# The second layer's feed-forward stage: a lower task rate in its first block, and wider spacing between the steps that write the first output rows

## The chip, the cores and the metric

The kernel runs on one core of one Trainium2 chip. The metric is the device time of one execution in microseconds; the time given for a kernel is the median of its runs. The profile is one further execution, recorded by the hardware profiler, with its own time and its own span from the first to the last instruction.

The core has TensorE (matrix products, with weight loads shown apart as PEld), VectorE (DVE), ScalarE (ACT), GpSimd (POOL) and SyncE (SP). Each works through its own list of instructions, and they wait for each other through semaphores. All transfers between HBM and the on-chip memory of this kernel are issued by SP, one after the other.

## The reference, cut to what matters

The reference is one inference step of a two-layer decoder, on a prompt of 1024 tokens and eight samples of eight tokens, 1088 token columns in all, with a model width of 1024. Each layer mixes tokens, adds the residual and normalises, then runs a feed-forward stage with its own residual and normalisation:

```python
def swiglu_ffn(x, w_in, w_out):
    gate, up = jnp.split(x @ w_in, 2, axis=-1)
    return (jax.nn.silu(gate) * up) @ w_out

xp = deepnorm_residual(xp, mix_p @ w_out[l], ln_mix_g[l], ln_mix_b[l])
xp = deepnorm_residual(xp, swiglu_ffn(xp, w_ffn_in[l], w_ffn_out[l]), ln_ffn_g[l], ln_ffn_b[l])
```

`deepnorm_residual(x, h, g, b)` is a layer norm over the 1024 features of `ALPHA * x + h`, with gain `g` and bias `b`. The hidden width is 2816. The samples' columns `xs` go through the same two lines. After layer 1 (the second) the result is the output `y`.

## The kernel before, in words

**Layout.** The residual stream `mx` is kept transposed: 128 features on the partitions, 8 feature tiles, and 1088 token columns. Columns are cut into three chunks: chunk 0 has 512, chunk 1 has 256 and chunk 2 has 320. To keep float32 accuracy every operand of a product is split into a high and a low part (`wh`, `wl` for weights, `xh`, `xl` for columns), and each product is three matmuls. ScalarE makes the high part of a weight (L169, in `halves`), and VectorE or GpSimd the low one (L172, which is the line of the helper `tt` and so stands for most VectorE and GpSimd work in the profile).

**The feed-forward stage** is `ffn(l, background)`, called once a layer. It has two blocks: block 0 takes chunk 0, block 1 takes chunks 1 and 2. A block goes through the 22 hidden tiles in six groups of four or three. For each hidden tile, `gates` makes seven products of sums of operands (a Strassen-like scheme) into PSUM, each 12 matmuls, and between them evacuates, applies the SiLU, multiplies, and writes the hidden tile `hid`. After each group, `parts` multiplies its hidden tiles with the output weights and `add_part` adds the results into `mx`. The four PSUM banks of one hidden tile come alternately from the pool `pd` (with one called `gp`) and from the pool `gb`. The sums of operands that a block needs are made by the task `combine_x`, which in block 1 may start only when block 0's last gates are done.

**The background tasks.** Work on vectors is written as Python generators, kept in a queue `S` (class `Streams`). The code that emits products calls `S.tick()` after every product of `gates` and after every `add_part`. A tick adds `S.rate` to a credit, and as many steps of tasks as the credit's whole part are emitted:

```python
self.credit = min(self.credit + self.rate, 2 * self.rate + 1)
if self.credit >= 1:
    self.credit -= self._advance(int(self.credit))
```

In one tick a task takes at most one step, tasks at the front first, and among the first three live tasks only. A task that yields `n` is due again `n` ticks later; one that yields 0 is due again at the next tick. A task that yields a condition isn't live until it holds. `S.until(cond)` steps tasks without emitting products until the condition holds.

Which instruction comes first on an engine is settled in two stages: the order in which the code emits it gives its priority, and a planner then places instructions by priority as they become ready, and gives out buffers from the pools.

**Tasks around the change.** `out_proj` queues `norm` for each chunk after the mixing. For chunks 1 and 2 (there `calm` is true) that task waits 14 ticks (`LAZY[0]`), adds up the eight feature tiles in four steps (`lnsum`), squares in four steps (`lnsq`), and after two waits scales the eight tiles in eight steps (L676). These tasks run beside block 0 of `ffn`. The rates are in `RT = (2.3, 3.0, 1.0, 4.25, 4.25, 2.5)`: the main program sets `RT[2]` before layer 0's output projection, which then holds through `ffn(0)`, and `RT[5]` before `ffn(1)`.

**The output rows.** In layer 1, block 1 begins by loading gain and bias rows (`grow`, `brow`) and queues `y_out(0, ...)`. It waits 14 ticks (`LAZY[1]`) and then handles chunk 0's four tiles of 128 tokens one by one through `y_tiles`: two halves, each four transposes into a PSUM bank `ytr`, statistics (L961) and a copy into the tile `yst`; then aggregate (L970), variance (L971) and its power on GpSimd; then two passes on VectorE for each half (L979, L982); then the store to `y_p` (L987) on SP's queue. `yst` comes from the pool `slots` of ten buffers, with the hidden tiles, `grow`, `brow` and part of the raw weights (`rawu`). Chunks 2 and 1 are handled by the same function at the end, without waits between steps. Weight loads are issued by `load_raw` (L249), on the same queue of SP as the stores.

Of the kernel before, what the change touches and what calls it, by code (L numbers as in the profile page):

```python
# [87 lines left out]
def trunk(ctx: ExitStack, tc: tile.TileContext, A: dict, O: dict, g128, g8):  # L88
# [35 lines left out]
    S = Streams(3)  # L124
    LNY = ((1, 5, 2), (3, 11, 5), (4, 7, 2))
    LAZY = (14, 14)
    RT = (2.3, 3.0, 1.0, 4.25, 4.25, 2.5)
# [43 lines left out]
    def tt(out, a, b, op, eng=None):  # L171
        (eng or nc.vector).tensor_tensor(out=out, in0=a, in1=b, op=op)  # L172
# [139 lines left out]
    def piece(ahead):  # L312
        prefetch(1)
        out = ready_pieces.popleft()
        prefetch(ahead)
        return out
# [508 lines left out]
    def ffn(l, background):  # L825
        def gates(blk, f, last):

            n = HALF[blk][1]
            XH, XL = x_sums(blk)
            assert plan[at["next"]][0] == ("sf", l, blk, f)  # L830
            at["next"] += 1

            def prod(i, ps, start, stop):
                wh, wl = piece(PA[0])
                for k in range(4):
                    mm(ps, lhsT=wl[:, k], rhs=XH[:, i, k], start=start and k == 0, stop=False, skip_group_check=True)
                    mm(ps, lhsT=wh[:, k], rhs=XL[:, i, k], start=False, stop=False, skip_group_check=True)
                    mm(ps, lhsT=wh[:, k], rhs=XH[:, i, k], start=False, stop=stop and k == 3, skip_group_check=True)
                S.tick()
                return ps  # L840

            sets["use"] ^= 1
            A_, B_, C_, D_ = (new_bank(i)[:, :n] for i in range(4))
            v, u1, u0 = (rt([P, n], nm) for nm in ("v1", "up1", "up0"))
            hid = slot([P, 2, 2 * n], F32R, "hid")

            def result(i, u, g):

                hs = slice(i * n, i * n + n)
                tt(g, u, g, ALU.mult)  # L850
                acopy(hid[:, 0, hs], g)
                tt(hid[:, 1, hs], g, hid[:, 0, hs].bitcast(F32), ALU.subtract)

            prod(0, A_, True, True)
            acopy(v, A_)
            prod(4, B_, True, True)
            tt(v, v, B_, ALU.add)
            prod(2, C_, True, True)
            tt(u1, v, C_, ALU.add)
            prod(1, D_, True, True)  # L860
            tt(u1, u1, D_, ALU.add)
            prod(3, A_, False, True)
            nc.scalar.activation(A_, A_, AF.Silu)
            prod(5, C_, False, True)
            tt(u0, v, C_, ALU.add)
            result(0, u0, A_)
            prod(6, D_, False, True)
            tt(D_, v, D_, ALU.add)
            nc.scalar.activation(D_, D_, AF.Silu)
            result(1, u1, D_)  # L870
            if last:
                done.add(("gates", l, blk))
            return hid

        def parts(outs, gi, hid, b0):

            sums = []
            for i, (w, m, c) in enumerate(outs):
                c0, n = CH[c]
                ps = new_bank(i)  # L880
                sums.append((w, ps[:, :n], slice(c0 - b0, c0 - b0 + n)))
            for ks in (range(len(hid) - 1), range(len(hid) - 1, len(hid))):
                for (wh, wl), ps, ts_ in sums:
                    for k in ks:
                        first, end = k == 0, k == len(hid) - 1
                        mm(ps, lhsT=wl[:, k], rhs=hid[k][:, 0, ts_], start=first, stop=False)
                        mm(ps, lhsT=wh[:, k], rhs=hid[k][:, 1, ts_], start=False, stop=False)
                        mm(ps, lhsT=wh[:, k], rhs=hid[k][:, 0, ts_], start=False, stop=end)
            for (w, m, c), (_, ps, _) in zip(outs, sums):
                add_part(ps, m, c, gi)  # L890

        def add_part(ps, m, c, gi):
            c0, n = CH[c]
            y = mx[:, m, c0:c0 + n]
            if gi == 0:
                nc.vector.scalar_tensor_tensor(out=y, in0=y, scalar=ALPHA, in1=ps, op0=ALU.mult, op1=ALU.add)
            else:
                tt(y, y, ps, ALU.add)
            S.tick()

        for blk in range(2):
            S.until(lambda: ("xsum", l, blk) in done)
            if l == 1 and blk == 1:
                grow, brow = slot([P, D], F32, "grow"), slot([P, D], F32, "brow")
                dma(grow, A["ln_ffn_g"][1:2, :].to_broadcast([P, D]))
                dma(brow, A["ln_ffn_b"][1:2, :].to_broadcast([P, D]))
                S.add(y_out(0, grow, brow))
            b0 = HALF[blk][0]
            for gi, (f0, f1) in enumerate(GROUPS):
                end = f1 == NF  # L910
                hid = []
                for f in range(f0, f1):
                    hid.append(gates(blk, f, f1 == NF and f == f1 - 1))
                    background()
                if end and blk == 1 and l == 0:
                    S.add(x_parts(0), front=True)
                for ci, cs in enumerate(LAST[l] if end and blk else (BCH[blk],)):
                    sums = [None, None]
                    for m in range(0, KT, 2):
                        ws = weights(("fo", l, blk, gi, ci, m))  # L920
                        outs = [(ws[q], m + q, c) for q in range(2) for c in cs]
                        if m == 0:
                            sets["use"] ^= 1
                            parts(outs[:4], gi, hid, b0)
                        for q in range(2):
                            for i, c in enumerate(cs):
                                if m or len(cs) * q + i >= 4:
                                    parts([(ws[q], m + q, c)], gi, hid, b0)
                                if end and l == 0 and blk:
                                    sums[i] = stat_add(sums[i], m + q, c, nc.vector)  # L930
                                elif end and (m + q) % 4 == 3:
                                    done.add(("y", c, m // 4))
                                    if blk and m < 4:
                                        S.add(y_out(c, grow, brow), front=True)
                    if end and l == 0:
                        for i, c in enumerate(cs):
                            S.add(norm(c, sums[i], 1, l), front=True)
# [10 lines left out]
    def y_tiles(c, tiles, grow, brow):  # L948
# [3 lines left out]
        for half in range(2):  # L952
            yield from wait(("y", c, half))
            hs = slice(half * 512, half * 512 + 512)
            for T, n in tiles:
                if half == 0:
                    st[T], st6[T] = slot([P, D], F32, "yst"), small(12, "yst6")
                b = bank("ytr")
                for i in range(4):
                    transpose(b[:n, i * P:(i + 1) * P], mx[:, half * 4 + i, T * P:T * P + n], ident)  # L960
                nc.vector.bn_stats(out=st6[T][:n, half * 6:half * 6 + 6], in_=b[:n])  # L961
                if end:
                    src[T, half] = b[:n]
                else:
                    acopy(st[T][:n, hs], b[:n])
                    src[T, half] = st[T][:n, hs]
                yield 0
        for T, n in tiles:
            mv, r = small(2, "ymv"), small(2, "yr")
            nc.vector.bn_aggr(out=mv[:n], in_=st6[T][:n].rearrange("p (a s) -> p a s", a=2))  # L970
# [3 lines left out]
        for T, n in tiles:  # L974
            mv, r = st6[T]
            for half in range(2):
                hs = slice(half * 512, half * 512 + 512)
                y, b = st[T][:n, hs], brow[:n, hs]
                nc.vector.scalar_tensor_tensor(out=y, in0=src[T, half], scalar=mv[:n, 0:1], in1=grow[:n, hs],  # L979
                                               op0=ALU.subtract, op1=ALU.mult)  # L980
                if half or c == 0:
                    nc.vector.scalar_tensor_tensor(out=y, in0=y, scalar=r[:n, 0:1], in1=b, op0=ALU.mult, op1=ALU.add)  # L982
                else:
                    nc.scalar.activation(y, y, AF.Copy, scale=r[:n, 0:1])
                    tt(y, y, b, ALU.add, nc.gpsimd)
            if T < 8:
                dma(O["y_p"][0, T * P:(T + 1) * P, :], st[T])  # L987
            else:
                dma(O["y_s"].rearrange("b t d -> (b t) d"), st[T][:64])
            yield 0  # L990
# [756 lines left out]
```

## Time and profile before

| What | Value |
|---|---|
| Median of 3 runs | 2698.9 us (2698.22 to 2705.96) |
| Profiled execution, its own time | 2692.69 us |
| Its span | 2690.9 us |
| Mean granted TensorE clock | 0.992 |
| Layer 1, block 0 of the feed-forward stage | about 1910 to 2247 us of the span |
| Layer 1, block 1 | about 2272 to 2664 us |
| Chunk 0's output rows on VectorE | 2298.5 to 2331 us |

Engine names in rows are PE and PEld (TensorE's products and weight loads), DVE, ACT, POOL and SP. In a row of busy time by stretch stand the stretch, its length, and each engine's busy time with the count of its instructions, then the granted clock, the share of the DMA engines and GB/s. A row of waits reads: the engine, the tile and line that waited, what released it, then the total in us, how often, and the longest. In a row of a group stand the line, engine, operation, tiles and shape with the count, then busy us and the mean ns of one, then the idle time before it. A row for one line or tile has the least, median and longest duration in ns, and the first and last start.

### The profile page before, as it was taken

How to read it: one execution, taken by the hardware profiler on the slowest of the kernel's cores; microseconds unless marked ns; L12 is line 12 of the kernel's file. 1: busy time of each engine (PE TensorE's matmuls, PEld its weight loads, DVE VectorE, ACT ScalarE, POOL GpSimd, SP SyncE). 2: the span in 40 equal slices, each digit the busy share in tenths (PEclk: the TensorE clock that was granted, in tenths of full speed). 3: DMA queues.
4: the chain of work that ended last, by engine and by line, in shares of the span. 5: the costliest groups of instructions: out<-in, count | busy, mean ns of one | idle time of the engine just before them, and what ended most of it. 6: DMA issues, size and time to landing. Idle time of an engine off the chain costs nothing. (4 is left out here: it accounts for less than half of the span.)

```text
span 2690.9 us, 48282 instructions
## 1 busy us (share of the span) xinstructions
PE 2603.3 (97%) x18057; PEld 2351.7 (87%) x18057; DVE 1829.9 (68%) x3843; ACT 1204.7 (45%) x2621; POOL 934.3 (35%) x1118
## 2 busy tenths in 40 slices
PE   8999999999999999999999999989999999899997
PEld 8788888898999989999977777768989998899997
DVE  4454435578777797665775775677887669866666
ACT  4442223344544554444455555544454445344434
POOL 0012223654444443334520111136344444433335
PEclk9999999999999999999999999989999999999998
DMA  7311111223333332333342453542333433433332
GB/s 253 95 41 49 49 56 57 64 86 126 114 120 116 122 114 89 120 114 94 103 132 61 146 163 95 160 141 87 102 99 126 134 110 122 134 114 114 99 98 83
DMA packets 417819, 289.23 MB, mean 107 GB/s; under 512 B 21360, under 2 KB 403120, under 8 KB 415920
## 3 DMA queue, kind: packets, MB, share of 16 engines
q1 hardware_dynamic: 417584, 286.13, 34.5%
q8 instruction: 143, 2.34, 0.3%
q14 instruction: 92, 0.75, 0.1%
HBM read 272.25 MB, written 40.83 MB: 116 GB/s over the span
## 5 line engine op out<-in xcount | busy, mean ns | idle before, releaser
L172 POOL TENSOR_TENSOR wl<-rawu,wh 128x256 fp32r<-128x256 f32 (+1 forms) x560 | 449.8, 828 | 833.1 <-ACT wh L169 744.9
L112 PE MATMUL pd<-xh,wl 128*128 128x256 f32 (+3 forms) x2080 | 673.8, 325 | 10.6 <-DVE up L172 3.9
L112 PE MATMUL pd<-xh,wh 128*128 128x256 f32 (+3 forms) x2080 | 660.3, 318 | 0.0
L112 PE MATMUL pd<-xl,wh 128*128 128x256 f32 (+3 forms) x2080 | 659.3, 317 | 0.2 <-DVE xl L172 0.2
L169 ACT ACTIVATE wh<-raw 128x512 fp32r<-128x512 f32 (+1 forms) x628 | 388.8, 623 | 565.6 <-DVE raw L172 206.0
L112 PEld LDWEIGHTS pd<-xh,wl 128*128 128x128 f32 x2080 | 392.8, 189 | 48.5 <-issue 21.3
L172 DVE TENSOR_TENSOR wl<-raw,wh 128x512 fp32r<-128x512 f32 x460 | 341.3, 745 | 120.1 <-ACT wh L169 116.2
L112 PEld LDWEIGHTS pd<-xl,wh 128*128 128x128 f32 x2080 | 394.5, 190 | 24.5 <-issue 5.8
L112 PEld LDWEIGHTS pd<-xh,wh 128*128 128x128 f32 x2080 | 392.7, 189 | 23.8 <-issue 4.4
L112 PE MATMUL gb<-xh,wl 128*128 128x256 f32 (+1 forms) x1232 | 356.6, 289 | 7.1 <-DVE up L172 3.3
L112 PE MATMUL gb<-xh,wh 128*128 128x256 f32 (+1 forms) x1232 | 355.6, 289 | 0.0
L112 PE MATMUL gb<-xl,wh 128*128 128x256 f32 (+1 forms) x1232 | 352.9, 286 | 0.0
L172 POOL TENSOR_TENSOR wl<-raw,wh 128x256 fp32r<-128x256 f32 x336 | 272.0, 836 | 128.4 <-ACT wh L169 115.5
L169 ACT ACTIVATE wh<-rawu 128x512 fp32r<-128x512 f32 (+1 forms) x280 | 170.8, 614 | 197.0 <-PE gb L112 81.2
L112 PE MATMUL gb<-hid,wh 128*128 128x320 f32 (+2 forms) x1056 | 251.8, 329 | 0.0
L112 PEld LDWEIGHTS gb<-xh,wl 128*128 128x128 f32 x1232 | 231.8, 188 | 10.1 <-DVE wl L172 3.2
L112 PE MATMUL pd<-hid,wh 128*128 128x256 f32 (+2 forms) x1018 | 240.3, 327 | 0.1
L112 PEld LDWEIGHTS gb<-xl,wh 128*128 128x128 f32 x1232 | 233.4, 189 | 0.6 <-DVE xl L172 0.2
L112 PEld LDWEIGHTS gb<-xh,wh 128*128 128x128 f32 x1232 | 231.5, 188 | 0.0
L112 PEld LDWEIGHTS gb<-hid,wh 128*128 128x128 f32 x1056 | 180.3, 189 | 13.9 <-DVE hid L172 0.3
L112 PEld LDWEIGHTS pd<-hid,wh 128*128 128x128 f32 x1018 | 172.5, 189 | 14.2 <-DVE hid L172 0.7
L112 PE MATMUL gb<-hid,wl 128*128 128x512 f32 (+2 forms) x528 | 174.0, 331 | 4.2 <-POOL wl L172 2.1
(321 smaller groups left out, 4724.0 us busy)
## 6 DMA issues: line engine op xcount, KB each, us to landing
rawu<-in_w_ffn_in_dram SPq DMA_DIRECT2D x88, 512.0 KB
raw<-in_w_ffn_in_dram SPq DMA_DIRECT2D x88, 512.0 KB
raw<-in_w_out_dram SPq DMA_DIRECT2D x32, 512.0 KB
raw<-in_w_ffn_out_dram SPq DMA_DIRECT2D x32, 512.0 KB
rawu<-in_w_ffn_out_dram SPq DMA_DIRECT2D x32, 512.0 KB
out_wins_dram<-in_cache_win_kv_g_dram SPq DMA_DIRECT2D x64, 256.0 KB
qb<-scr_q SPq DMA_DIRECT2D x64, 256.0 KB
raw<-in_w_in_a_dram SPq DMA_DIRECT2D x26, 512.0 KB
```

What stands on the lines that cost most here:

```text
L112: return pinned(nc.tensor.matmul(*args, **kw))
L169: nc.scalar.activation(out, in_, AF.Copy, scale=scale)
L172: (eng or nc.vector).tensor_tensor(out=out, in0=a, in1=b, op=op)
```

## The change

Two things are edited. In `ffn`, each block now sets the rate after its operands are there: `RT[5]` = 2.5 in block 1 of layer 1 and `RT[2]` = 1.0 elsewhere. Since `ffn(0)` already ran at 1.0, this alters block 0 of layer 1 alone, from 2.5 to 1.0. In `y_tiles`, for chunk 0 alone, a half that has been transposed is followed by a pause of 4 ticks where it was 0, and a pause of 4 ticks is added after each half's last two passes, ahead of the store.

```diff
         for blk in range(2):
             S.until(lambda: ("xsum", l, blk) in done)
+            S.rate = RT[5] if l and blk else RT[2]
             if l == 1 and blk == 1:
...
                     acopy(st[T][:n, hs], b[:n])
                     src[T, half] = st[T][:n, hs]
-                yield 0
+                yield 4 if c == 0 else 0
         for T, n in tiles:
...
                     nc.scalar.activation(y, y, AF.Copy, scale=r[:n, 0:1])
                     tt(y, y, b, ALU.add, nc.gpsimd)
+                if c == 0:
+                    yield 4
             if T < 8:
                 dma(O["y_p"][0, T * P:(T + 1) * P, :], st[T])
```

## The prediction

> **What bounds the kernel now.** I read the page's totals first, then the busy time by stretch, then TensorE's list of waits in the stretches where it is not full.
>
> ```profile
> span 2690.9 us, 48282 instructions
> PE 2603.3 (97%) x18057; PEld 2351.7 (87%) x18057; DVE 1829.9 (68%) x3843; ACT 1204.7 (45%) x2621; POOL 934.3 (35%) x1118
> ```
>
> TensorE sets the end, so only its holes can be won. The change touches layer 1's feed-forward stage alone, and its two blocks begin at about 1910 and 2272 us. The first row below lies in layer 1's first block, the second at the same work in layer 0, the third in layer 1's second block where the first rows of output are made, the fourth just behind it.
>
> ```profile
> core 0: us, PE busy (x) PEld busy (x) DVE busy (x) ACT busy (x) POOL busy (x), PEclk, DMA share, GB/s
> 1936.00:2012.00 76.00, 65.08 (x431) 59.09 (x430) 63.90 (x121) 37.15 (x81) 32.90 (x40) 0.98 0.32 100
> 632.00:708.00 76.00, 71.64 (x488) 65.97 (x487) 66.18 (x131) 40.16 (x88) 33.20 (x40) 0.98 0.36 114
> 2298.00:2336.00 38.00, 31.14 (x225) 29.17 (x225) 35.31 (x67) 16.36 (x33) 19.81 (x21) 1.00 0.48 153
> 2336.00:2400.00 64.00, 64.00 (x485) 64.00 (x484) 41.92 (x81) 27.45 (x53) 23.18 (x30) 1.00 0.36 115
> ```
>
> TensorE is idle for 76 − 65.08 = 10.92 us in layer 1's first block, for 4.36 us at the same work in layer 0, and for 38 − 31.14 = 6.86 us beside the output rows. VectorE is 93% busy in that third stretch. With VectorE at 41.92 / 64 = 65%, TensorE has no hole. So the two holes worth having are 10.9 and 6.9 us. What ends them, in the same order (layer 1's first block, layer 0's, the output rows):
>
> ```profile
> PE pd L112 <- DVE up L172: 3.5, 2, 2.1
> PE lnm L112 <- DVE lnsum L172: 2.9, 2, 2.6
> PE pd L112 <- ACT hid L169: 2.3, 1, 2.3
> PE pd L112 <- POOL wl L172: 2.2, 1, 2.2
> ```
> ```profile
> PE gb L112 <- POOL wl L172: 1.9, 1, 1.9
> PE gb L112 <- DVE up L172: 1.2, 2, 0.9
> PE gb L112 <- ACT hid L169: 0.6, 1, 0.6
> ```
> ```profile
> PE gb L112 <- DVE up L172: 1.9, 1, 1.9
> PE pd L112 <- POOL wl L172: 1.5, 1, 1.5
> PE pd L112 <- ACT hid L169: 1.3, 1, 1.3
> PE gb L112 <- ACT yst L169: 1.1, 1, 1.1
> PE gp L112 <- DVE up L172: 1.0, 1, 1.0
> ```
>
> In each, the products wait for evacuations and weight parts that stand behind other work on VectorE. No DMA is among the releasers.
>
> **Part 1: the pace in the first block.** At each tick the queue of tasks gets `rate` steps of credit. In layer 1's first block the rate falls from 2.5 to 1.0, which is what layer 0 has throughout. The live tasks there are the two `norm` tasks of chunks 1 and 2 alone; `combine_x(1, 1)` waits for the last gates, and with one live task whose steps are one tick apart, either rate gives one step a tick. At 2.5 both norms step at every tick; at 1.0 they share one step. No operation is added or removed. What it spreads is seen in VectorE's timeline and in the norms' scaling at L676, layer 1 first and then layer 0:
>
> ```profile
> 1942.18 3.67 DVE L172 TENSOR_TENSOR lnsum<-lnsum,mx 128x256 f32<-128x256 f32 x4
> ```
> ```profile
> L676 DVE SCALAR_TENSOR_TENSOR mx<-mx,lnp,lnb x16: 469/505/544, 1995.5 to 2011.6; 128x256 f32<-128x256 f32 x8, 128x320 f32<-128x320 f32 x8
> ```
> ```profile
> L676 DVE SCALAR_TENSOR_TENSOR mx<-mx,lnp,lnb x16: 466/508/547, 683.6 to 710.5; 128x256 f32<-128x256 f32 x8, 128x320 f32<-128x320 f32 x8
> ```
>
> Four sums in a row hold VectorE for 3.67 us, and the same 16 scalings take 16.1 us in layer 1 and 26.9 us in layer 0. After the change the two layers have the same tasks, the same pace and the same tick positions here, so layer 0 is the forecast. That equal emission gives equal timing is not only argued: where `combine_x` runs at the turn of the blocks, both layers already agree to a hundredth.
>
> ```profile
> 915.00:985.00 70.00, 66.58 (x465) 62.46 (x464) 64.59 (x112) 38.77 (x77) 30.80 (x36) 1.00 0.37 116
> 2226.00:2296.00 70.00, 66.57 (x466) 62.46 (x465) 64.59 (x111) 38.70 (x77) 30.30 (x36) 1.00 0.42 137
> ```
>
> Gain: 10.92 − 4.36 = 6.56, say **6.5 us**. The ends: 10.9 if every hole goes, and 0 if the holes only move, each step still meeting the same products later. A loss I exclude: the norms end some 11 us later at most (26.9 − 16.1), and what needs them starts at about 2245 us, over 200 us behind. The work that hides the moved sums is the block's own products; without that cover the two norms' 16 scalings, 8 us, would stand open.
>
> **Part 2: the output rows of chunk 0.** Before, a tile takes three ticks: half 0, half 1, finish and store (`yield 0` means the next tick, since a task steps once a tick). After, it takes 4 + 4 + 4 + 4 + 1 = 17, so four tiles take 68 instead of 12, from tick 15 of the block to tick 82. What is emitted stays the same, four stores on SP's queue included. VectorE's part of it, in the groups of 2298 to 2332 us:
>
> ```profile
> L982 DVE SCALAR_TENSOR_TENSOR yst<-yst,yr,brow 128x512 f32<-128x512 f32 x8 | 8.6, 1106 | 1.8 <-POOL yr L172 1.8
> L979 DVE SCALAR_TENSOR_TENSOR yst<-yst,ymv,grow 128x512 f32<-128x512 f32 x8 | 6.2, 805 | 0.0
> L961 DVE BATCH_NORM_STATS2 yst<-ytr 128x6 f32<-128x512 f32 x8 | 5.5, 692 | 0.5 <-PE ytr L115 0.5
> L970 DVE BATCH_NORM_AGGREGATE ymv<-yst 128x2 f32<-128x12 f32 x4 | 0.8, 205 | 0.0
> L971 DVE TENSOR_SCALAR yr<-ymv 128x1 f32<-128x1 f32 x4 | 0.6, 150 | 0.0
> ```
>
> Together 8.6 + 6.2 + 5.5 + 0.8 + 0.6 = 21.7 us. How long a tick is, and what VectorE has left in the gates, come from the chain of waits and from one later group of four gates:
>
> ```profile
> 2354.43 11.11 PE gb L112 x84
> ```
> ```profile
> 2424.40:2468.90 44.50, 44.50 (x339) 44.50 (x338) 31.39 (x62) 23.52 (x46) 18.08 (x24) 1.00 0.40 127
> ```
>
> One hidden block is 84 matmuls and seven ticks, so a tick is 1.59 us. VectorE's own load is 31.39 / 44.5 = 71%. Twelve ticks are 19 us and leave 0.29 × 19 = 5.6 us for 21.7 us of work, so 16 us run over and TensorE pays 6.86 of them. Sixty-eight ticks are 108 us, and 21.7 / 108 adds 20%: about 91% in the gates. That fits but is not idle. The nearest row for TensorE beside a VectorE so loaded, from layer 0's norms:
>
> ```profile
> 680.00:720.00 40.00, 39.02 (x316) 37.92 (x315) 37.34 (x80) 28.47 (x61) 16.68 (x21) 1.00 0.38 123
> ```
>
> At 93% TensorE loses 0.98 of 40 us, 2.4%. Of the 68 ticks, 42 fall into gates (15 to 28 and 45 to 72, with 16 ticks of output parts between), 67 us, so 1.6 us stay. Layer 0's first turn from gates to output parts in its second block, with norms beside it, waits 0.8 us:
>
> ```profile
> PE gb L112 <- ACT hid L169: 0.8, 1, 0.8
> ```
>
> I keep that too. Gain: 6.86 − 1.6 − 0.8 = **4.4 us**. The ends: 6.9, and −2 if each of the eight transposed halves costs TensorE the 1.1 us that one cost above (`gb <- ACT yst`: a PSUM buffer of the gates still held by the transposed rows). I take the middle because tick positions speak against the low end: tiles 0 and 3 transpose in gates that use the other PSUM pool, tile 1 in the output parts, and only half 0 of tile 2, at tick 49, meets the pool it needs; before, half 1 of tile 2 and all of tile 3 did. The tile's buffer is held 17 ticks instead of three, in a pool of ten with four hidden tiles, `grow`, `brow` and the second halves of weight loads. That is ten in use at the fullest point (three hidden tiles, two output weights, one gate weight, `grow`, `brow`, one output tile, the fourth hidden tile), so I cost it at nothing. Without that last free buffer a weight load slips by one hidden block, 11 us.
>
> The clock. In both first blocks the granted clock falls once:
>
> ```profile
> 640.00:650.00 10.00, 8.05 (x47) 7.36 (x46) 7.56 (x16) 6.19 (x16) 7.24 (x11) 0.83 0.39 117
> 1940.00:1950.00 10.00, 6.46 (x32) 5.48 (x33) 8.29 (x15) 2.98 (x6) 3.80 (x4) 0.83 0.08 25
> 1950.00:1960.00 10.00, 7.76 (x57) 7.16 (x56) 9.37 (x18) 8.04 (x22) 7.71 (x10) 1.00 0.26 81
> 1960.00:1970.00 10.00, 7.73 (x45) 6.52 (x45) 8.98 (x16) 4.17 (x11) 7.70 (x9) 1.00 0.45 130
> ```
>
> Mean 0.83 over 10 us is 1.7 us of work lost. Layer 0's falls at its hole of 1.9 us, layer 1's at its hole of 2.6 us, so the comparison keeps one dip and the sum has none for it.
>
> **The sum.** 6.5 + 4.4 = 10.9 us. The profiled execution took 2692.69 us (span 2690.9), so 2681.8 there. The median of the runs is 2698.9, 0.23% above it; the same gain from it gives **2688.0 us**, −0.40%.
>
> **The rivals.**
> (a) Only the pace pays: the output rows' wait is spread with the rows, and TensorE pays as much in many small pieces. For it: 91% is close to full, and each tile still puts several operations in front of an evacuation. Against: at 93% the row above shows 2.4%, not 18%. 2698.9 − 6.5 = 2692.4.
> (b) The clock dip goes too. Mechanism: the dip came at one hole of 1.9 us, while the rows at 1.00 above hold layer 1's waits of 2.2 and 2.3 us. So length alone doesn't decide, and the hole of 1.9 us that stays may escape, though in layer 0 the same sequence of holes did not. Then 1.7 us more are won: 2686.3.
> [...]
> (c) No change: the planner that places instructions by readiness puts the spread work where it was. Against: layer 0's 26.9 against 16.1 us. 2698.9.
> (d) Slower: stores in front of weight loads. SP's queue is one line, and a store waits for its L982 there.
>
> ```profile
> SPq L987 <- DVE yst L982: 19.0, 2, 16.5
> ```
> ```profile
> 2324.94 0.79 SPq L249 DMA_DIRECT2D rawu<-in_w_ffn_in_dram  x1
> ```
> ```profile
> 2331.82 0.81 DVE L172 TENSOR_TENSOR s<-raw,rawu 128x512 f32<-128x512 f32 x1
> ```
>
> One store held the queue for 16.5 us. Behind the stores, the tightest weight load was issued 6.9 us ahead of its use. From a hold of 6.9 us on, TensorE waits. The spread rows span two turns of gates and output parts with such loads; if a store sits ahead of each for 16.5 us, 2 × (16.5 − 6.9) = 19.2 us are lost and 10.9 won: 2707.2. Against: the long hold came from rows that VectorE could not finish, and now a store follows its last operation by four ticks, 6.3 us.
>
> **How the numbers follow.** Forecast 0.53, its own range 2684 to 2692; (b) 0.18; (a) 0.16; (c) 0.07; (d) 0.06. What a measurement of this kernel can tell from no change is 0.3%, 8 us, so faster means under 2690.8. Of the forecast 0.46 lies below that, of (b) all, of (a) 0.02: 0.66. Within: the rest of the forecast 0.07, of (a) 0.13, (c) 0.07: 0.27. Slower: (d), and 0.01 of (a): 0.07. The range leaves out (d), and half of (c): 2682 to 2698.
>
> **What would show it.** Right: TensorE's idle time at layer 1's first sums and scalings near 4.4 us, its L676 stretched to about 27 us, no run of four `lnsum` in one piece, output rows of chunk 0 from about 2292 to 2400 us with TensorE idle under 3 us there, and stores that wait on SP only a few us. Wrong: L676 still within 16 us; holes `gb <- ACT yst` in each tile; or DMA as TensorE's or VectorE's releaser after a long wait of L987.

## The result, and the profile after

The changed kernel takes 2684.8 us (median of six runs) beside 2702.7 us for the kernel before on the same chip: a ratio of 0.9945, 95% interval 0.9935 to 0.9956, so 14.9 us faster (11.9 to 17.6). A second comparison, on another occasion, gave 0.9932 (0.9914 to 0.9949). The forecast was 2688.0 us and a gain of 10.9 us: the sign and the two places were right, the sizes were not.

The two profiled executions do not show this at first sight: 2692.69 us before, 2690.33 after, a difference of only 2.4 us. The reason lies ahead of the change. These are rows of busy time by stretch for the code between layer 0's first matmul with 288 columns and the last matmul of layer 1's output projection, where TensorE's list of instructions is the same in both kernels; before first, then after (columns: stretch, length, PE, PEld, DVE, ACT and POOL busy with their counts, granted clock, DMA share, GB/s).

```profile
956.30:1909.90 953.60, 921.65 (x6481) 800.27 (x6480) 676.04 (x1586) 465.52 (x1127) 302.19 (x349) 0.99 0.38 115
```
```profile
956.70:1922.50 965.80, 929.79 (x6480) 808.12 (x6480) 674.80 (x1586) 465.59 (x1127) 302.48 (x349) 0.98 0.38 113
```

The same work took 12.2 us longer in the profile of after: 8.1 us in TensorE's busy time, at a lower clock (0.98 beside 0.99), and 4.1 us in its holes. In eleven further profiles below, this stretch lies anywhere between 955 and 967 us. So stages must be compared, not spans. Three matmuls mark layer 1's feed-forward stage in TensorE's timeline: the last one of the output projection, the first with 288 columns, and the last pair on hidden tiles (start, duration). Before, then after:

```profile
1909.85 0.31 PE L112 MATMUL po<-mixh,wh 128*128 128x320 f32 x1
...
2267.82 0.30 PE L112 MATMUL pd<-xh,wl 128*128 128x288 f32 x1
...
2672.75 0.40 PE L112 MATMUL pd<-hid,wh 128*128 128x256 f32 x2
```
```profile
1922.50 0.31 PE L112 MATMUL po<-mixh,wh 128*128 128x320 f32 x1
...
2274.81 0.30 PE L112 MATMUL pd<-xh,wl 128*128 128x288 f32 x1
...
2670.89 0.40 PE L112 MATMUL pd<-hid,wh 128*128 128x256 f32 x2
```

The second of the last pair starts 0.12 us after the first. By these marks the second block begins at 2267.8 us and ends at 2672.9 us in the profile of before, a little off the round figures of the table of before. The first block goes from 2267.82 − 1909.85 = 358.0 us to 352.3, a gain of 5.7. The second goes from 2672.87 − 2267.82 = 405.05 us to 396.2, a gain of 8.8. The tail behind it, to the end of the span, is 0.4 us shorter (18.0 to 17.6). Together that is 15.0 us, which is what the timed runs show.

Inside the blocks, these rows of after answer to those shown of before. First the busy time: the first block, layer 0's block at the same work, and the stretch of the output rows in two parts.

```profile
1948.00:2024.00 76.00, 69.80 (x480) 64.85 (x479) 65.04 (x131) 39.20 (x85) 32.53 (x40) 0.98 0.35 112
632.00:708.00 76.00, 71.63 (x488) 65.96 (x487) 66.04 (x131) 39.76 (x87) 33.21 (x40) 0.98 0.37 116
2300.00:2360.00 60.00, 60.00 (x458) 59.99 (x457) 46.17 (x88) 25.61 (x50) 25.03 (x32) 1.00 0.37 116
2360.00:2412.00 52.00, 52.00 (x395) 51.78 (x394) 43.16 (x83) 24.55 (x49) 24.07 (x29) 1.00 0.44 142
```

TensorE is idle for 6.2 us where it was 10.9 before and is 4.4 in layer 0. Beside the output rows it has no hole left, with VectorE 77% and 83% busy. What TensorE still waits for in the first block, how the scaling is spread, and what the output rows cost VectorE:

```profile
PE pd L112 <- POOL wl L172: 3.3, 1, 3.3
PE pd L112 <- DVE up L172: 1.9, 2, 1.7
PE pd L112 <- DVE wl L172: 1.0, 1, 1.0
```
```profile
L676 DVE SCALAR_TENSOR_TENSOR mx<-mx,lnp,lnb x16: 463/506/543, 2001.9 to 2028.8; 128x256 f32<-128x256 f32 x8, 128x320 f32<-128x320 f32 x8
```
```profile
L983 DVE SCALAR_TENSOR_TENSOR yst<-yst,yr,brow x8: 736/806/1233, 2316.5 to 2399.4; 128x512 f32<-128x512 f32 x8
L971 DVE BATCH_NORM_AGGREGATE ymv<-yst x4: 193/206/210, 2311.8 to 2394.4; 128x2 f32<-128x12 f32 x4
L990 SPq DMA_DIRECT2D out_y_p_dram<-yst x4: 357/363/572, 2320.9 to 2406.8; - x4
```

The wait of the norm's own matmul for four sums in a row (`lnm <- lnsum`, 2.9 us before) is gone. The 16 scalings take 26.9 us, exactly layer 0's length. The output rows, between 2298 and 2331 us before, now run from 2305 to 2407 us. VectorE's line numbers are shifted by one there (L982 is L983), and the store is L990.

### The profile page after: what moved, and what is told of

The parts are those of the page before. It is cut to its first block, busy times and chain, and to the rows that moved or that the text cites. A ratio compares the mean times of both kernels' runs of the same rounds, so it can differ in the third digit from the quotient of the medians.

```text
span 2688.6 us, 48291 instructions
## 1 busy us (share of the span) xinstructions
PE 2608.4 (97%) x18057; PEld 2359.0 (88%) x18057; DVE 1823.9 (68%) x3843; ACT 1204.4 (45%) x2621; POOL 930.7 (35%) x1118
## 5 line engine op out<-in xcount | busy, mean ns | idle before, releaser
L112 PE MATMUL gb<-xl,wh 128*128 128x256 f32 (+1 forms) x1232 | 353.2, 287 | 0.0
```

The costliest lines, as they stand in the source:

```text
L112: return pinned(nc.tensor.matmul(*args, **kw))
```

## The experiments

Every kernel is the changed one with the edit shown, except where the kernel before is named. Times of stages are taken from the three matmuls above. "Stage" is the whole, from the last matmul of the output projection to the last on hidden tiles. The kernels with pauses after halves, pauses after passes and pauses of 2, with the pools swapped and with a rate of 0.5 in layer 1 alone were run once each, for the profile; their stages rest on that one execution.

| Kernel | First block | Second block | Stage |
|---|---|---|---|
| before | 358.0 | 405.05 | 763.0 |
| changed | 352.3 | 396.2 | 748.5 |
| pace alone | 353.5 | 404.65 | 758.2 |
| spacing alone | 358.0 | 396.2 | 754.2 |
| pauses after halves | 352.3 | 397.9 | 750.2 |
| pauses after passes | 353.5 | 398.1 | 751.55 |
| pauses of 2 | 352.4 | 397.4 | 749.8 |
| pools swapped | 352.1 | 398.5 | 750.6 |
| rate 0.5, layer 1 | 353.25 | 394.9 | 748.2 |
| rate 0.5, both layers | 353.2 | 394.9 | 748.1 |
| sums later | 352.7 | 396.2 | 748.9 |
| before, again | 358.0 | 408.4 | 766.4 |
| changed, again | 352.3 | 396.2 | 748.5 |

**The two parts alone.** The pace alone takes both pauses back out; the spacing alone drops the new line.

```diff
-                yield 4 if c == 0 else 0
+                yield 0
-                if c == 0:
-                    yield 4
```

> The new rate alone; the output rows of chunk 0 keep their three ticks a tile. If the two parts add up (each stage pays for its own bunched VectorE work), layer 1's first block, from the last matmul of the output projection to the first matmul with 288 columns, takes 352.3 us as in the changed kernel (358.0 before), the second block 405.0 as before, and the run is 5.7 us (0.21%) faster than before. If the first block's work only helps because the second is spread too, the first block stays near 358.

```diff
-            S.rate = RT[5] if l and blk else RT[2]
```

> The spacing of the output rows alone, with the rate of 2.5 throughout layer 1's feed-forward stage. If the parts add up: first block 358.0 us, second block (first matmul with 288 columns to the last on hidden tiles) 396.2 us where before it took 405.0; 8.8 to 9.3 us (0.34%) faster than before. If the second block's gain came from a better start out of the first, it is under 7 us.

Measured: the pace alone 0.9964 (0.9951 to 0.9977), first block 353.5 us and second block 404.65; the spacing alone 0.9953 (0.9938 to 0.9967), first block 358.0 and second 396.2. By stages each part does its own block's work and leaves the other's alone, so the parts add: 758.2 − 763.0 = −4.9 and 754.2 − 763.0 = −8.8, together −13.7 of −14.5. The first block's missing 1.2 us with the pace alone stand beside a longer dip of the clock there (0.72 over 10 us, where the changed kernel has 0.83; second row below). The kernel with pauses after passes, whose first block has the same edit, shows the same pair: 353.5 us and 0.66 over 10 us. The first row is the dip of the second block:

```profile
2320.00:2330.00 10.00, 8.06 (x49) 7.68 (x48) 7.45 (x13) 2.46 (x4) 6.83 (x9) 0.83 0.78 231
1950.00:1960.00 10.00, 6.64 (x33) 5.96 (x33) 8.28 (x16) 5.67 (x15) 7.06 (x10) 0.72 0.32 92
```

By timed runs, each part is worth more than its stage shows: 9.7 us (6.2 to 13.2) and 12.7 us (8.9 to 16.8). The next experiment bears on that.

**The same two kernels again.** The kernel before and the changed kernel under new names, beside the same runs of before, with no edit.

> The kernel before once more under another name, to see what a comparison gives for no change: the ratio holds 1.0, and layer 1's feed-forward stage takes 763.0 us. If the code ahead of the change is what varies between profiles, the stretch from layer 0's first matmul with 288 columns to the last of layer 1's output projection lies anywhere between 953 and 967 us again, though its instructions are the same.

> The changed kernel once more, beside the same runs of before: the ratio is again about 0.9945 (15 us), layer 1's feed-forward stage takes 748.5 us, and the two parts measured alone (0.9964 and 0.9953) are then known to add up to less than their sum of 22 us, within their intervals of 3.5 and 4 us.

Measured: the kernel before gave 1.0002 (0.9989 to 1.0015), the changed one 0.9932 (0.9914 to 0.9949). The changed kernel's stage repeats to a tenth (748.5 us). The kernel before's does not: its second block took 408.4 us where it was 405.05, at the same code. Two dips of the clock stand there, beside holes of the output rows that are a little different in this execution (`gp <- up` 2.5 us instead of 1.0):

```profile
2310.00:2320.00 10.00, 7.49 (x48) 7.26 (x48) 9.56 (x17) 3.94 (x8) 4.45 (x4) 0.83 0.33 107
2340.00:2350.00 10.00, 8.58 (x49) 7.72 (x48) 6.29 (x15) 3.01 (x6) 3.93 (x6) 0.83 0.61 178
```
```profile
PE gp L112 <- DVE up L172: 2.5, 1, 2.5
PE gb L112 <- DVE up L172: 1.9, 1, 1.9
PE pd L112 <- POOL wl L172: 1.9, 1, 1.9
PE pd L112 <- ACT hid L169: 1.3, 1, 1.3
```

A mean of 0.83 over 10 us is at most 1.7 us of TensorE's work (an estimate, 0.17 × 10), less where a dip lies partly in a hole, as the first one does. Taken from start to start (each gap between the starts of two matmuls in the trace, less the median gap of that shape), 2.6 of the 3.4 us (408.4 − 405.05) stand in matmuls that follow each other later without showing idle time, and 0.75 in longer holes. The three profiles that still bunch the rows (before, before again, pace alone) have none, two and one such dip in the second block; none of the ten profiles with spread rows has one (1.00 in the changed kernel's two rows above). So in these profiles the holes cost their own length and, in two of the three, a fall of the clock to 0.83 beside them, and the profile of before that the forecast was made from was one without. That is seen in three profiles only. It accounts for part of the surplus of the timed runs over the stages: set against this profile's 766.4 us, the pace alone is worth 8.2 us by stage and the spacing alone 12.2, and both lie inside the intervals of the timed runs. How often the timed runs of before had such dips isn't known. The stretch ahead of the stage was 961.7 us in the repeated kernel before and 956.2 in the repeated changed one, within the 953 to 967 expected.

**Why the spread rows cost nothing: load, bursts or banks.** Three variants keep the pace and cut the pauses: after the transposed halves alone, after the last passes alone, and everywhere but 2 ticks long.

```diff
-                if c == 0:
-                    yield 4
```

> As the changed kernel, but the pauses stand after the transposed halves alone: a tile takes 4 + 4 + 1 = 9 ticks, and its four last passes (about 3.9 us of VectorE) are again emitted in one step. Load theory (what counts is VectorE's work over the ticks that the rows span): 36 ticks, of which 16 lie in output parts where VectorE is half free, leave about 21 us for 21.7 us of work: second block 396 to 398.5 us. Burst theory (what counts is how much one step puts in front of an evacuation): four bursts at about 1 us each, about 400 us. Bank theory (a transposed half in gates that use the same PSUM pool costs 1.1 us): tile 1's two halves fall there, about 398.5 us.

```diff
-                yield 4 if c == 0 else 0
+                yield 0
```

> As the changed kernel, but the pauses stand after each half's last passes alone: a tile takes 1 + 1 + 4 + 4 + 1 = 11 ticks. Load theory: 44 ticks leave more than the 21.7 us needed, second block 396 to 397 us. Burst theory: the largest step is now two passes, 396 to 397 us. Bank theory: the halves of tile 1 (ticks 26, 27) and tile 3 (48, 49) fall into gates that use the same PSUM pool, four times 1.1 us, about 400.6 us.

```diff
-                yield 4 if c == 0 else 0
+                yield 2 if c == 0 else 0
...
-                    yield 4
+                    yield 2
```

> As the changed kernel with pauses of 2 ticks instead of 4: 2 + 2 + 2 + 2 + 1 = 9 ticks a tile, so the same 36 ticks as with pauses after the halves alone, but no step larger than two passes. Load theory: the same as there, second block 396 to 398.5 us. Burst theory: clearly less than there, about 396.5 us. The changed kernel has 396.2, the kernel before 405.0.

Measured, second block: 397.9, 398.1 and 397.4 us. TensorE's waits beside the output rows are, in the same order:

```profile
PE gb L112 <- DVE v L172: 1.4, 1, 1.4
```
```profile
PE pd L112 <- DVE up L172: 0.6, 1, 0.6
PE pd L112 <- DVE mx L896: 0.4, 1, 0.4
```
```profile
PE gb L112 <- DVE v L172: 0.4, 1, 0.4
PE pd L112 <- ACT hid L169: 0.3, 1, 0.3
```

The bank theory falls: with pauses after the passes the transposes of tiles 1 and 3 lie among matmuls into `gb`, the pool in question, as was forecast, and no wait for a copied half (`<- ACT yst`) appears; 398.1 is not 400.6. The burst theory falls at the size that I gave it: four passes in one step cost 397.9, not 400, and splitting them at the same 36 ticks saves 0.5 us, not 1.4. The load theory gives the size of all three within its bounds except for pauses after the passes, which came out at 398.1 instead of 396 to 397 although its 44 ticks are the longest of the three. Why two holes of 0.4 and 0.6 us are left there is open. In short: going from 12 to 36 ticks wins 7.2 to 7.7 of the 8.8 us, and going on to 68 wins the other 1.2 to 1.7.

**What is left in the first block.** Layer 0 takes 351.1 us at the same work, layer 1 now 352.3. The pools of PSUM banks alternate, and layer 1 starts with the other one.

```diff
+        sets["use"] ^= l
         for blk in range(2):
             S.until(lambda: ("xsum", l, blk) in done)
```

> As the changed kernel, but layer 1's feed-forward stage starts with the other PSUM pool, as layer 0 does (the pools alternate with each hidden tile, and layer 0 makes an odd number of turns, so layer 1 starts with the other one). If that is what keeps layer 1's first block at 352.3 us where layer 0 takes 351.1, it takes 351.1 here. If the rest is something else (the rate of the output projection ahead of it, the loads), it stays at 352.3.

Measured: 352.1 us. The waits become layer 0's almost one by one (`wl` on GpSimd 1.9, `hid` 0.6, 0.4, 0.2), but the first one doesn't:

```profile
PE gb L112 <- DVE up L172: 2.0, 2, 1.7
PE gb L112 <- POOL wl L172: 1.9, 1, 1.9
PE gb L112 <- ACT hid L169: 0.6, 1, 0.6
PE pd L112 <- DVE up L172: 0.4, 1, 0.4
PE pd L112 <- DVE wl L172: 0.2, 1, 0.2
```

So the pool decides which holes there are (3.3 us or 1.9 at the first turn to output parts), while the length of the block hardly changes, and the second block, whose pools are swapped too, is 2.3 us longer. The first hole, 1.7 us here and 0.9 in layer 0, is not explained; neither the rate of the output projection nor the loads, the other two rivals, were varied.

**Spreading the norms further.** A rate of 0.5 in layer 1's first block, then in both layers', and, in another kernel, a longer first pause of the norms.

```diff
-            S.rate = RT[5] if l and blk else RT[2]
+            S.rate = (RT[5] if blk else 0.5) if l else RT[2]
```

> As the changed kernel, with a rate of 0.5 in layer 1's first block. Load theory: the norms' steps are spread over about twice the ticks, and most of the 6.3 us of TensorE's holes left there go: first block 348 to 350 us. If what is left is set by positions (the first turn from gates to output parts, whose weight parts wait on GpSimd), it stays at 351 to 352.5. If late norms delay the sums of operands for the second block, it gets longer than 352.3.

```diff
-            S.rate = RT[5] if l and blk else RT[2]
+            S.rate = (RT[5] if blk else 0.5) if l else (RT[2] if blk else 0.5)
```

> As the changed kernel, with a rate of 0.5 in the first block of both layers. Load theory: layer 0's first block, 351.1 us so far, falls to 348 to 350 as layer 1's does, and the run is 3 to 6 us faster than the changed kernel (0.66 to 0.77% faster than before). If positions set what is left, it is equal to the changed kernel, 0.55% faster than before.

```diff
-    LAZY = (14, 14)
+    LAZY = (27, 14)
```

> As the changed kernel, with the norms' first pause 27 ticks instead of 14 in both layers, so that their sums begin in the output parts of the first group (eight ticks of about 2.7 us, VectorE half free) and not in the last two hidden tiles ahead of them. Place theory (what is left in the first block is the sums standing in front of the last gates and of the first output weights): the holes of the first block fall from 6.3 to about 3 us in layer 1 and from 4.5 to about 2 in layer 0; layer 1's feed-forward stage, from the last matmul of the output projection to the last on hidden tiles, goes from 748.5 to about 745.5 us; 5 us faster than the changed kernel. If the waits at the first turn are there whatever stands beside them, the holes stay and it is equal to the changed kernel.

Measured: with 0.5 in layer 1 the stage takes 748.2 us; with 0.5 in both layers 748.1, layer 0's first block 350.8, and the ratio is 0.9957 (0.9941 to 0.9973); with the later sums 748.9, and 0.9937 (0.9922 to 0.9952). Neither of the two timed kernels differs from the changed one beyond the intervals. The 350.8 us are no gain either: the profile of the pace alone, which leaves layer 0 as it was, has 349.8 us, with the clock at 1.00 from 640 to 650 us where the changed kernel's profile, with 351.1 us, has 0.83. The scalings did spread at 0.5, over 75 us:

```profile
L676 DVE SCALAR_TENSOR_TENSOR mx<-mx,lnp,lnb x16: 471/504/543, 2014.1 to 2088.7; 128x256 f32<-128x256 f32 x8, 128x320 f32<-128x320 f32 x8
```

But the holes came back elsewhere. TensorE's waits in the first block at a rate of 0.5, and with the later sums:

```profile
PE lnb L112 <- DVE mx L172: 2.2, 1, 2.2
PE pd L112 <- DVE up L172: 1.3, 1, 1.3
PE pd L112 <- DVE hid L172: 1.2, 1, 1.2
PE pd L112 <- ACT hid L169: 0.7, 1, 0.7
PE gp L112 <- DVE up L172: 0.6, 1, 0.6
```
```profile
PE lnb L112 <- DVE lnd L665: 3.7, 2, 3.5
PE gb L112 <- DVE up L172: 1.9, 2, 1.4
PE pd L112 <- DVE up L172: 1.4, 1, 1.4
```

Their sums are 6.0 and 7.0 us, against 6.2 in the changed kernel. The longest is now the norm's own matmul (`lnb`), which waits for VectorE while the products behind it in TensorE's list wait with it; whether those could have run isn't shown. The load theory and the place theory both fall for the first block: six to seven us of holes stay, at a rate of 1.0 or 0.5 and at either place. What 0.5 costs in the first block, 0.9 us, comes back in the second, which is 1.3 us shorter: two holes of 1.2 and 1.5 us at its start, which the profiles of before and of the changed kernel both have, shrink to 1.4 us together. So no version here beats the changed kernel by more than 0.4 us of the stage.

## Why the prediction was right, and where not

**Part 1, the pace: right, 5.7 us for 6.5.** Layer 0 as the forecast held in its mechanism: the same length of the scalings (26.9 us), the burst of sums gone, and no loss from later norms. In idle time, the forecast's own measure, the gain is 4.7 us (10.9 to 6.2). The step that was a little off is that layer 0's holes carry over whole. Tasks and pace are the same, but the PSUM pools are not, and the first product's hole is 1.7 us instead of 0.9. The pools decide which of the later holes there are; they are not the cause of the difference, since with them swapped the first hole is still 1.7 us and the block 352.1 us. That cause is open. The agreement at the turn of the blocks, shown to a hundredth, did not carry over to a place with other pools.

**Part 2, the output rows: right in sign, 8.8 us for 4.4.** The terms that were mis-sized are "1.6 us stay" and "0.8 us stay": both are 0. VectorE was put at about 91% in the gates. In the changed kernel it is 88% busy in the gates from 2305.2 to 2324.0 us, 68% in the output parts behind them and 83% in the next gates (2350.4 to 2396.8 us), and TensorE has no hole in any of the three. The loss of 2.4% came from a stretch at 93%, with waits for evacuations and a weight part (`up` 0.4 and 0.3 us, `wl` 0.2); why that stretch has them and 88% has none isn't shown. The second error is the size of the hole itself. A hole counts from the end of a matmul's busy time, but a product's matmuls start 132 ns apart (84 in 11.11 us), while one is busy for 309 ns:

```profile
L112 PE MATMUL gb<-xh,wl 128*128 128x288 f32 x28 | 8.6, 309 | 3.0 <-DVE up L172 1.9 <-ACT yst L169 1.1
```

By an estimate from these two figures, each hole therefore costs about 309 − 132 = 177 ns more than it shows: for seven holes (the five listed, and two under 0.1 us in the trace) 1.2 us. The block gained 8.84 − 6.86 = 2.0 us more than its holes. The remaining 0.8 us are in the trace too: taken from start to start, delays too short to show as idle time add up to 3.3 us in the second block before and 2.5 us after.

**The buffer and the bank at nothing: right.** With 17 ticks of holding no DMA became a releaser of TensorE. VectorE waited for a load once, 0.6 us, which it did not before. No wait for a copied half is left.

**The clock: half right.** The dip in the first block stayed, as the sum had it:

```profile
1960.00:1970.00 10.00, 7.39 (x44) 7.00 (x45) 7.40 (x15) 6.50 (x17) 6.72 (x9) 0.83 0.54 160
```

What the forecast left out is the clock beside the holes of the output rows, none to two dips in the three profiles with bunched rows, or 0 to 3.4 us at the estimate of 1.7 us for each. Rival (b), 2686.3 us, was near the measured time by other means: its dip did not go. Its doubt was sound all the same: in the profile of the pace alone layer 0's code is unchanged, its hole of 1.9 us is there, and no dip follows (1.00 from 640 to 650 us, where the profile of before has 0.83).

**Rivals (a), (c) and (d).** (a) is refuted by the second block's lost holes, (c) by both blocks. (d) is refuted at its own point of decision. A store did hold SP's queue, for longer than the 6.9 us that were named, against the forecast's "only a few us", and TensorE had no hole:

```profile
SPq L990 <- DVE yst L983: 22.0, 2, 12.8
```

So the lead of that one load was not the margin of the ones behind the moved stores.

**The sum and the base.** 10.9 us against 15.0 by stages. In idle time alone the sum is close, 4.7 + 6.9 = 11.6 us, but by luck: the first part was put 1.8 us too high and the second 2.4 too low. The forecast was set on a median of 2698.9 us from three runs; six runs gave 2702.7, and eleven, twelve and seventeen further ones 2699.4, 2702.3 and 2704.2. This too helped the forecast of the time: from 2702.7 the same gain would have given 2691.8 us, 7 us above the measured 2684.8. The profiled execution, 2692.69 us, lay below them, mostly by the stretch ahead of the stage (953.6 us, where the others took 955 to 967).

## What to carry to other kernels

In this kernel TensorE sets the end, and spreading VectorE's bunched side work won 5.7 us in one block and 8.8 us in the other; look for stretches where an engine is nearly full and the one that sets the end has holes, and give its side work more ticks. Here the holes were there with VectorE 93% busy and gone at 68 to 88%, but the first block kept 6.2 us of holes at 86%, so the share alone doesn't decide. Compare one stage between two profiles by its first and last instruction, not the spans: here unchanged code differed by 12 us, while the changed kernel's stage repeated to 0.1 us. Profile the kernel before twice as well: its stage differed by 3.4 us. And count a hole from start to start of the matmuls, since busy records hide part of what it costs (here 309 ns busy beside 132 ns from start to start). Spreading has an end: once VectorE had room, half the pace or another place left about as many us of holes in the first block (6.0 and 7.0 beside 6.2).

## What the runs showed of the hardware

- The granted clock fell behind short holes. In the repeated kernel before, no wait listed in the second block's bunched rows is over 2.5 us, and the clock fell twice to a mean of 0.83 over 10 us. In layer 0 of the profile of before, TensorE is idle for 1.95 us between 642 and 645 us, with products before and behind; the clock is 1.00 up to 645 us, 0.50 from 646 to 648 us, and 1.00 again from 649 us.
- Whether such a dip comes varied between executions of the same code: none (1.00 from 2272 to 2664 us) and two (0.83, the rows above) in the second block of the kernel before. Behind layer 0's hole of 1.9 us a dip follows in the profile of before (0.83 from 640 to 650 us) and none in the profile of the pace alone (1.00). What decides it isn't shown.
- The last pass of an output row (`yst<-yst,yr,brow`) has the same shape in both kernels and a mean of 1106 ns when bunched and 934 ns when spread:

```profile
L983 DVE SCALAR_TENSOR_TENSOR yst<-yst,yr,brow 128x512 f32<-128x512 f32 x8 | 7.5, 934 | 0.1
L980 DVE SCALAR_TENSOR_TENSOR yst<-yst,ymv,grow 128x512 f32<-128x512 f32 x8 | 7.2, 908 | 0.0
```

The pass ahead of it goes the other way, from 805 to 908 ns, so that the sum is about the same (14.8 and 14.7 us).
